# A hybrid decoder layer on one core: first steps in a fixed order, small products in larger groups, attention inputs between other projections

## The chip, the core and the metric

The kernel runs on one core of a Trainium2 chip, in one launch. The metric is the device time of a whole execution in microseconds (us). The core's engines are TensorE (PE in the profile; PEld is its weight load, PEq and SPq the sequencers), VectorE (DVE), ScalarE (ACT), GpSimd (POOL) and SyncE (SP), which here only issues DMAs. A step of the program becomes instructions in one queue per engine; an engine works its queue in order and waits on semaphores of the others.

## The reference

One decoder layer of width 1024 on one sequence of 256 tokens, all in float32:

```
h    = rms_norm(x, norm1_g)
proj = h @ w_in                                  # 1024 x (1824 + 1536 + 2048)
z    = token shift of proj[:1824]                # z + mu * (z of the token before - z)
y_a  = rwkv7_time_mix(z, ...)                    # 8 heads of 64: a recurrence over the tokens
q, k = partial_rope(rms_norm(.)); v              # from proj[1824:3360], 8 heads of 64
y_b  = softmax(causal q k^T / 8) v
g_a, g_b = sigmoid(proj[3360:])                  # two gates of 1024
x    = x + (g_a * (y_a @ w_branch_a) + g_b * (y_b @ w_branch_b)) @ w_out
x    = x + conv_ffn(rms_norm(x, norm2_g))        # up 1024 x 5632, conv of 3, gelu, down 2816 x 1024
```

The recurrence is, for each head, with a 64x64 state S: `S = S*w + (S a) b^T + v k^T`, `y = S r`, with w, a, b, k from the projections. Attention has blocks of 256 tokens, so with 256 tokens it is plain causal attention.

## The kernel before

**Weights and products.** All matrices of weights (some 68 MB) are read once, in tiles `raw` of 128 x 1024 (512 KB), by DMAs on SP's queue (`load_next`, L234), four buffers deep. Each tile is split into a high half `whi` in a shorter format of the same width, fp32r (`split_hi`, L239: a cast on ScalarE, L246, but for the first tile and those numbered 4 to 6, which VectorE casts: `HI_ENG`, L50), and a low half `wlo` (`split_lo`, L251, a subtraction on VectorE, L256). The activations are split in the same way into `hh` and `hl`. A product is then three: `hh`x`whi`, `hl`x`whi`, `hh`x`wlo`. `wst` (L275) has the weights stationary and 256 columns moving (L284, L286, L289), `xst` (L294) the activations stationary and 512 columns of weights moving (L305, L306, L309). These are called weight products below; a tile of weights gives 24 or 12 of them. Whoever takes a tile (`weights`, L261) also splits the next ones and so starts the next load.

**The first steps.** The gains of the norm (`p0`) and x come by DMA. ScalarE squares x, takes the root; VectorE takes the reciprocal `rs`, and x is multiplied by it (L333 to L342); TensorE transposes the result into PSUM (`xt`), from which ScalarE makes `hh` with the gains `par` as scale (L357) and VectorE `hl` (L358). `keep_warm` gives TensorE idle products (`idle`, L99). `ident` comes from an iota on POOL (L105). The other parameters follow: `p1` on SP's queue behind the first four weights, the rest on POOL's queue (`small_loads`), then the masks `gmask`, `cmask`, `m16`, `m32` and constants (`late_consts`, VectorE) and the tables of the rotation (`rope_tables`).

**Threads.** Up to branch 1 three kinds of work are merged. `bulk` (L949) makes the projections, each as one run of weight products: the decay and gate inputs first, then k, r, v of the recurrence, the three inputs of attention (`finish_qk` norms and rotates q and k), eight gates, and, when attention is done, branch 1. `chain` (L486) is the recurrence in four chunks of 64 tokens: decay (`pw`), normalisation of k (`pss`, `rx`, `prx`), the products of all chunks' keys with keys and queries (`pgr`, 8 heads x 4 chunks as 16 units x 2 halves of the partitions), masked into `G` (L595); then the inverse of a unit triangular matrix 64x64 for each unit. Its 16x16 diagonal blocks go through DRAM (`d`) into another layout, are inverted in fifteen steps on VectorE (L609 to L614) and come back through DRAM as `X` (L617, L623); two levels (`level`, L692) join them to 32 and 64. Meanwhile `pk`, `pv`, `pz0` prepare transposes and products that don't need `X`. Then the four chunks run one behind the other (`pz`, `pu`, `pS`, `pyt`), and `group_norm` (L733) follows each with `pc`. `attention` (L849) transposes q and k, makes the scores (`ps`), the softmax (L879 to L893), transposes it (`ppt`) and multiplies by v (`po`), in four parts: two halves of the tokens (t) by two halves of the heads (j), and writes `ybh` and `ybl`, which branch 1 takes (L917, L918).

**What sets the order.** `chain`, `bulk`, `attention` and `group_norm` are generators. Each `yield cost, latency` says how much of TensorE's time the step took and how long the thread should wait until its next one; the loop at L968 runs the first thread that is due, and `SLACK` scales the latencies. This gives the order in which instructions are written. A scheduler then may change each engine's order, by its own model, but for what `tc.issue_after` pins. A product of weights has 128 rows; most products of `chain` and `attention` have 64 rows on either half of the array, and the two kinds alternate on TensorE wherever a step of a thread falls between weight products.

After the threads come branch 0, the output projection and the MLP, which keep their code.

Of the kernel before, what the change touches and what calls it, by code (L numbers as in the profile page):

```python
# [9 lines left out]
F32 = mybir.dt.float32  # L10
# [8 lines left out]
S = 256  # L19
# [17 lines left out]
def body(tc, x, positions, norm1_g, w_in, rwkv_mu, w_decay_up, decay_bias, w_aaa_up,  # L37
# [5 lines left out]
    with ctx:  # L43
# [6 lines left out]
        HI_ENG = {i: dve for i in (4, 5, 6)}  # L50
# [37 lines left out]
        p0 = t1("p0", (8, 128))  # L88
        nc.gpsimd.dma_start(p0, rows(norm1_g, 8))
        x_sb = load_x()  # L90

        ones = cst.tile([128, 512], mybir.dt.bfloat16, name="ones")
        dve.memset(ones, 1.0)

        def keep_warm(n):

            p = acc("idle")
            for _ in range(n):
                pe.matmul(p, ones[:, 0:128], ones, start=True, stop=True)  # L99

        keep_warm(8)
        jp = t1("jp", (128, 128), I32)
        pool.iota(jp, pattern=[[1, 128]], base=0, channel_multiplier=-1)
        ident = cst.tile([128, 128], F32, name="ident")
        pool.tensor_scalar(ident, jp, 0.0, None, op0=OP.is_equal)  # L105
        eps1 = cst.tile([128, 2], F32, name="eps1")
        dve.memset(eps1[:, 0:1], NORM_EPS)
        dve.memset(eps1[:, 1:2], GN_EPS)
        warm = cst.tile([128, 1], F32, name="warm")
        act.activation(warm, eps1[:, 0:1], AF.Sqrt)  # L110
        jl = t1("jl", (128, 2, 64), I32)
        for q in range(2):
            pool.iota(jl[64 * q:64 * q + 64], pattern=[[0, 2], [1, 64]], base=0,
                      channel_multiplier=-1)
        p1 = t1("p1", (51, 128))
        p1_loads = []
        at = 0
        mu1 = rwkv_mu[0]
        for r, n in ((mu1[0:1792].rearrange("(n c) -> n c", c=128), 14),
                     (mu1[1696:1824].rearrange("(n c) -> n c", c=128), 1),  # L120
                     (rows(decay_bias, 4), 4), (rows(aaa_bias, 4), 4), (rows(k_k, 4), 4),
                     (rows(k_a, 4), 4), (r_k[0].rearrange("h n -> (h n)").rearrange("(n c) -> n c", c=128), 4),
                     (rows(ln_g, 4), 4), (rows(ln_b, 4), 4), (rows(norm2_g, 8), 8)):
            p1_loads.append((p1[at:at + n], r))
            at += n
        assert at == 51
        p2 = t1("p2", (88, 128))

# [8 lines left out]
        def late_consts():  # L137
            dve.tensor_scalar(gmask[:, 0:64], jl[:, 0], 0.0, None, op0=OP.is_gt)
            dve.tensor_scalar(gmask[:, 64:128], jl[:, 1], 0.0, None, op0=OP.is_ge)
            dve.memset(bones, 0.0)  # L140
            for q in range(2):
                dve.memset(bones[64 * q:64 * q + 64, 64 * q:64 * q + 64], 1.0)
            dve.tensor_reduce(rowf, ident.rearrange("p (a b c) -> p a b c", a=4, b=2)[:, :, 1, :],
                              axis=AX.XY, op=OP.add)
            dve.memset(m16, 0.0)
            dve.memset(m32, 0.0)
            for q in range(4):
                o = 32 * (q % 2)
                dve.memset(m16[32 * q:32 * q + 32, o:o + 16], 1.0)
                if q % 2:  # L150
                    dve.memset(m32[32 * q:32 * q + 32, 0:32], 1.0)
            dve.tensor_scalar(m16, m16, rowf, None, op0=OP.mult)
            dve.tensor_scalar(cmask, jp, 0.0, NEG, op0=OP.is_gt, op1=OP.mult)
            dve.memset(rst, 1.0)
            dve.memset(rst.rearrange("p (c i) -> p c i", i=64)[:, :, 0:1], 0.0)

# [3 lines left out]
        pt = atp("pt")  # L160
        pe.transpose(pt[:, 0:8], p0, ident[:8, :8])
        keep_warm(3)
# [3 lines left out]

        def late_params():
            pt = atp("pt")
            pe.transpose(pt[:, 0:51], p1, ident[:51, :51])
            pe.transpose(pt[:, 64:152], p2, ident[:88, :88])  # L170
            dve.tensor_copy(par[:, 8:59], pt[:, 0:51])
# [54 lines left out]

        queue, raws, halves, ready = [], [], [], []

        def load_next():
            if queue:  # L230
                ap = queue.pop(0)
                k, c = ap.shape[1], ap.shape[2]
# [892 lines left out]
```

## Time and profile before

| | us |
|---|---|
| runs | 438.62, 438.62, 439.71 (median 438.62) |
| the profiled execution | 438.61 |
| its span, first to last instruction | 436.8 |

| engine | busy of the span | instructions |
|---|---|---|
| PE (matmul) | 97% | 3600 |
| DVE | 69% | 545 |
| ACT | 56% | 391 |
| POOL | 3% | 21 |

The granted clock of TensorE is full in all 40 slices of the span. The core reads 68.76 MB at a mean of 161 GB/s. The times of the page and of the trace are counted from the span's start; of the 438.61 us, 1.8 lie around it. In a row of a group, `out<-in` names the tiles, then come the partitions x elements and the type, the count, the busy time with the mean of one in ns, and the idle time ahead of it with what ended most of it. Matmuls are pipelined, so the busy time of one is longer than the step from one to the next; where this matters, starts are compared. Where the costliest groups stand:

```profile
L284 PE MATMUL acc<-hh,whi 128*128 128x256 f32 x600 | 150.1, 284 | 1.7 <-ACT whi L246 0.8
L256 DVE TENSOR_TENSOR wlo<-raw,whi 128x1024 fp32r<-128x1024 f32 x125 | 152.2, 1219 | 53.1 <-PE acc L289 18.4
```

The first is one of the three kinds of weight products, 600 of them; the second the low halves on VectorE, which stood idle for 53.1 us before them.

### The profile page before, as it was taken

The page shows a single profiled execution, that of the slowest core. Times are in us where ns is not written, and L with a number is a line of the kernel's source. Part 1 is how long each engine was busy: PE and PEld are TensorE (multiplying, and loading weights), DVE is VectorE, ACT ScalarE, POOL GpSimd, SP SyncE. Part 2 cuts the span into 40 slices and gives each one's busy share as a digit, 9 for nine tenths or more (in the row PEclk, how much of TensorE's full clock was granted, in tenths as well). Part 3 has the DMA queues.
Part 4 walks back from the last instruction along what each step waited for, and adds up shares of the span by engine and source line. Part 5 has one row for each costly group of instructions (what it writes and reads, how often), then busy time and mean ns, then how long its engine had stood idle before and what let it go on. Part 6 is the DMA issues. An engine that isn't in the chain of part 4 may idle for free.

```text
span 436.8 us, 8837 instructions
## 1 busy us (share of the span) xinstructions
PE 425.6 (97%) x3600; PEld 384.0 (88%) x3600; DVE 301.4 (69%) x545; ACT 243.0 (56%) x391; POOL 12.8 (3%) x21
## 2 busy tenths in 40 slices
PE   7799998999999999999999999999999999999996
PEld 3688996788899989799997899999999999999995
DVE  4695899698456568676796479576576576576573
ACT  6489852644375446777355378455455455465450
POOL 6000040000000000000000000000000000000000
PEclk9999999999999999999999999999999999999999
DMA  8764836543657331164556366655665656565612
GB/s 234 195 190 125 243 94 195 132 129 54 194 154 230 95 104 51 50 190 127 166 182 195 107 211 184 226 189 166 200 192 178 195 193 191 191 182 185 214 50 96
DMA packets 62189, 70.76 MB, mean 162 GB/s; under 512 B 8898, under 2 KB 52617, under 8 KB 62150
## 3 DMA queue, kind: packets, MB, share of 16 engines
q1 hardware_dynamic: 61750, 69.50, 53.1%
q0 software_dynamic: 400, 0.71, 0.6%
q8 instruction: 28, 0.46, 0.4%
q14 instruction: 11, 0.09, 0.1%
HBM read 68.76 MB, written 1.44 MB: 161 GB/s over the span
## 4 chain that ended last, share of the span: by engine, by line
PE 82%; DVE 5%; ACT 5%; DMA 4%; issue 1%; SPq 1%; DVEq 0%; ACTq 0%
PE acc L284 15%; PE acc L286 15%; PE acc L289 15%; PE acc L305 4%; PE f L1045 4%; PE f L1043 4%; PE f L1044 4%; PE acc L306 4%; PE acc L309 4%; DMA raw<-in_w_in_dram 4%; DVE wlo L256 2%; ACT whi L246 1%; PE ps L876 1%; PE pp L704 1%; PE py L720 1%
## 5 line engine op out<-in xcount | busy, mean ns | idle before, releaser
L246 ACT CAST whi<-raw 128x1024 fp32r<-128x1024 f32 x121 | 126.4, 1050 | 119.3 <-PE acc L286 52.6
L256 DVE TENSOR_TENSOR wlo<-raw,whi 128x1024 fp32r<-128x1024 f32 x125 | 152.2, 1219 | 53.1 <-PE acc L289 18.4
L284 PE MATMUL acc<-hh,whi 128*128 128x256 f32 x600 | 150.1, 284 | 1.7 <-ACT whi L246 0.8
L286 PE MATMUL acc<-hl,whi 128*128 128x256 f32 x600 | 148.7, 282 | 0.9 <-DVE hl L358 0.9
L284 PEld LDWEIGHTS acc<-hh,whi 128*128 128x128 f32 x600 | 113.1, 188 | 4.4 <-ACT hh L357 1.5
L286 PEld LDWEIGHTS acc<-hl,whi 128*128 128x128 f32 x600 | 113.1, 188 | 3.2 <-DVE hl L358 1.5
L289 PE MATMUL acc<-hh,wlo 128*128 128x256 f32 x600 | 95.1, 281 | 1.2 <-DVE wlo L256 1.2
L289 PEld LDWEIGHTS acc<-hh,wlo 128*128 128x128 f32 x600 | 80.9, 189 | 2.1 <-DVE wlo L256 2.0
L1044 PE MATMUL f<-whi,hb 128*128 128x512 f32 x80 | 31.1, 389 | 0.0
L1043 PE MATMUL f<-whi,hb 128*128 128x512 f32 x80 | 31.1, 389 | 0.0
L1045 PE MATMUL f<-wlo,hb 128*128 128x512 f32 x80 | 31.1, 389 | 0.0
L305 PE MATMUL acc<-whi,hh 128*128 128x512 f32 x48 | 20.2, 425 | 0.0
L306 PE MATMUL acc<-whi,hl 128*128 128x512 f32 x48 | 18.8, 393 | 0.0
L1058 DVE TENSOR_TENSOR an<-acc,rsb 128x512 f32<-128x512 f32 x11 | 7.6, 691 | 14.8 <-PE acc L289 13.9
L1045 PEld LDWEIGHTS f<-wlo,hb 128*128 128x128 f32 x80 | 15.0, 188 | 3.1
L1044 PEld LDWEIGHTS f<-whi,hb 128*128 128x128 f32 x80 | 15.0, 188 | 2.7
L1043 PEld LDWEIGHTS f<-whi,hb 128*128 128x128 f32 x80 | 15.0, 188 | 2.7
L1076 DVE TENSOR_TENSOR cv<-cv,acc 128x256 f32<-128x256 f32 x22 | 8.3, 418 | 11.5 <-PE acc L289 11.2
L309 PE MATMUL acc<-wlo,hh 128*128 128x512 f32 x48 | 15.0, 393 | 0.0
L1065 ACT ACTIVATE cv<-an,cpar 128x256 f32<-128x256 f32 x22 | 12.0, 594 | 1.4 <-DVE an L1058 0.4
L305 PE MATMUL acc<-whi,mh 128*128 128x512 f32 x32 | 12.8, 399 | 0.0
L306 PE MATMUL acc<-whi,ml 128*128 128x512 f32 x32 | 12.6, 395 | 0.0
(274 smaller groups left out, 566.1 us busy)
## 6 DMA issues: line engine op xcount, KB each, us to landing
raw<-in_w_ffn_up_dram SPq DMA_DIRECT2D x44, 512.0 KB
raw<-in_w_in_dram SPq DMA_DIRECT2D x43, 512.0 KB
raw<-in_w_ffn_down_dram SPq DMA_DIRECT2D x22, 512.0 KB
raw<-in_w_out_dram SPq DMA_DIRECT2D x8, 512.0 KB
x<-in_x_dram SPq DMA_DIRECT2D x8, 256.0 KB
raw<-in_w_branch_b_dram SPq DMA_DIRECT2D x4, 512.0 KB
raw<-in_w_branch_a_dram SPq DMA_DIRECT2D x4, 512.0 KB
out_dram<-o SPq DMA_DIRECT2D x3, 256.0 KB
```

What stands on the lines that cost most here:

```text
L246: act.copy(hi[:, :k * c], raw[:, :k * c])
L256: dve.tensor_tensor(lo[:, :n], raw[:, :n], hi[:, :n].bitcast(F32), op=OP.subtract)
L284: pe.matmul(om, wh[:, k, ms], xh[:, k0 + k], start=k0 + k + m == 0, stop=False, skip_group_check=True)
L286: pe.matmul(om, wh[:, k, ms], xl[:, k0 + k], start=False, stop=False, skip_group_check=True)
L289: pe.matmul(om, wl[:, k, ms], xh[:, k0 + k], start=False, stop=k0 + k == nk - 1 and m == n - 1, skip_group_check=True)
L305: pe.matmul(ps_[t], xh[:, K, ts], wh[:, k], start=K == 0, stop=False)
L306: pe.matmul(ps_[t], xl[:, K, ts], wh[:, k], start=False, stop=False)
L309: pe.matmul(ps_[t], xh[:, K, ts], wl[:, k], start=False, stop=K == nk - 1)
L1043: pe.matmul(fin[f], hb[:, 0, i, ts], wh[:, 0, cs], start=st, stop=False)
L1044: pe.matmul(fin[f], hb[:, 1, i, ts], wh[:, 0, cs], start=False, stop=False)
L1045: pe.matmul(fin[f], hb[:, 0, i, ts], wl[:, 0, cs], start=False, stop=False)
L1065: act.activation(cv, pm, AF.Identity, scale=cpar[:, 44 + n:45 + n], bias=cpar[:, 66 + n:67 + n])
```

## The change

**The first steps** are written as one function, `first_steps`, under a fixed order (`tc.manual_schedule`) for PE, ACT, DVE and POOL. The factor `rs` of the norm is no longer multiplied into x: TensorE multiplies x by a diagonal matrix, `diag`, which transposes and scales in one. The gains and the first parameters come in one tile `p1` on POOL's queue (five issues), and no parameters go over SP's any more; the first weight tile is loaded in two halves. The order of the first weights' products is written out: high with `hh`, then `hl`, for four rows of weights, and their low halves behind; the first low half is made on POOL (`split_lo(pool)`), and `HI_ENG` is gone. The sigmoid's table is loaded ahead by a dummy. `late_consts` moves from VectorE to POOL, but for two instructions, `masks`, which are written in `chain`; the rest of the parameters are read out of `p2` by `late_params`, inside `chain`.

**Larger groups.** `pw`, `pgr`, `pk`, `pv`, `pz0` take four (`pv`, `pz0`: two) banks of PSUM at a time, and one step does what two or four did. `pk` now stands ahead of `pgr`. The two threads `level` become four joint steps for both halves. `pS` and `pyt` of a chunk are one step. `pc` of `group_norm` waits until a step of another thread than `bulk` has just been taken (`joined`). Attention does the first half of the tokens for all eight heads at once and the second half in two times four heads, and multiplies by v for each half of the tokens in one go (`weighted`).

**Order.** The inputs of attention stand between the other projections, and the first gate of branch 1 too; the planner's latencies are set anew, without `SLACK`.

```diff
-        HI_ENG = {i: dve for i in (4, 5, 6)}
+        joined = [False]
...
         def late_consts():
-            dve.tensor_scalar(gmask[:, 0:64], jl[:, 0], 0.0, None, op0=OP.is_gt)
...
+            pool.memset(rst, 1.0)
+            pool.memset(rst.rearrange("p (c i) -> p c i", i=64)[:, :, 0:1], 0.0)
+            pool.memset(wgu[0:96, 1], 0.0)
+            pool.memset(bones, 0.0)
             for q in range(2):
-                dve.memset(bones[64 * q:64 * q + 64, 64 * q:64 * q + 64], 1.0)
+                pool.memset(bones[64 * q:64 * q + 64, 64 * q:64 * q + 64], 1.0)
+            pool.tensor_scalar(gmask[:, 0:64], jl[:, 0], 0.0, None, op0=OP.is_gt)
+            pool.tensor_scalar(gmask[:, 64:128], jl[:, 1], 0.0, None, op0=OP.is_ge)
+            pool.tensor_scalar(cmask, jp, 0.0, NEG, op0=OP.is_gt, op1=OP.mult)
+            pool.memset(m16, 0.0)
+            pool.memset(m32, 0.0)
+            for q in range(4):
+                o = 32 * (q % 2)
+                pool.memset(m16[32 * q:32 * q + 32, o:o + 16], 1.0)
+                if q % 2:
+                    pool.memset(m32[32 * q:32 * q + 32, 0:32], 1.0)
+
+        def masks():
             dve.tensor_reduce(rowf, ident.rearrange("p (a b c) -> p a b c", a=4, b=2)[:, :, 1, :],
                               axis=AX.XY, op=OP.add)
...
             dve.tensor_scalar(m16, m16, rowf, None, op0=OP.mult)
...
-        queue += kh(win, 1536, 256) + kh(win, 1696, 128)
-        for c in (512, 768, 0, 256, 1024, 1280):
-            queue += kh(win, c, 256)
-        for i in range(3):
-            queue += kh(win, MOBA0 + 512 * i, 512)
...
+        for c, n in ((512, 256), (768, 256), (0, 256), (256, 256), (MOBA0, CW), (1024, 256), (1280, 256),
+                     (MOBA0 + CW, CW), (GATE0 + D, 256), (MOBA0 + 2 * CW, CW), (GATE0 + D + 256, 256),
+                     (GATE0 + D + 512, 256), (GATE0 + D + 768, 256)):
+            queue += kh(win, c, n)
...
+        def first_steps():
...
+            for i in range(NRAW):
+                load_next(i == 0)
...
+            keep_warm(8)
+            first_loads()
+            pool.iota(jp, pattern=[[1, 128]], base=0, channel_multiplier=-1)
+            pool.tensor_scalar(ident, jp, 0.0, None, op0=OP.is_equal)
...
+            small_loads(5)
...
+            for t in range(2):
...
+                act.activation(rs[:, t:t + 1], ss[:, t, 1:2], AF.Sqrt, scale=1.0 / D, bias=ss[:, t, 0:1])
+                dve.reciprocal(rs[:, t:t + 1], rs[:, t:t + 1])
+                diag = t1("diag", (128, 128))
+                dve.tensor_scalar(diag, ident, rs[:, t:t + 1], None, op0=OP.mult)
+                for k in (0, 2, 1, 3, 4, 6, 5, 7):
+                    pe.matmul(at(k)[:, t], x_sb[t][:, k * 128:k * 128 + 128], diag, start=True, stop=True)
+                if t == 0:
+                    pt = atp("pt")
+                    pe.transpose(pt[:, 0:31], p1, ident[:31, :31])
+                    early_params(pt)
+                    keep_warm(2)
...
+            for k in range(6):
+                high(k)
+            for k in range(2):
+                dve.tensor_copy(hi[:, k * 512:k * 512 + 512], raw[:, k * 512:k * 512 + 512])
+                low(k)
+            split_lo(pool)
+            small_loads(len(loads))
+            split_hi()
+            high(6)
+            high(7)
+            for k in range(2, 8):
+                low(k)
+            split_lo()
+            split_hi()
+            p = acc()
...
+            act.activation(warm, eps1[:, 0:1], AF.Sigmoid)
+            split_hi()
+            return p
...
+        with tc.manual_schedule(engines={E.PE, E.Activation, E.DVE, E.Pool}):
+            p = first_steps()
+        late_consts()
...
+            masks()
+            for g in range(2):
+                pg = [[p.rearrange("p (u i) -> p u i", u=4) for p in pj] for pj in banks("pgr")]
+                for ct in (2 * g, 2 * g + 1):
+                    for c in range(4):
...
+                for ct in (2 * g, 2 * g + 1):
+                    for q in range(2):
+                        dve.tensor_tensor(G[q][:, 4 * ct:4 * ct + 4], pg[ct % 2][q],
+                                          gmask[:, None, :].to_broadcast([128, 4, 128]), op=OP.mult)
...
-            for t, j in ((0, 0), (0, 1), (1, 0), (1, 1)):
...
+            p0 = yield from scores(0, 0, 8)
+            yield weighted(0, p0)
+            pa = yield from scores(1, 0, 4)
+            pb = yield from scores(1, 1, 4)
+            yield weighted(1, pa + pb)
...
-            for i in range(3):
+            def attention_input(i):
...
+            rope_tables()
+            yield from attention_input(0)
+            yield from proj4("v", 8)
+            yield from attention_input(1)
+            yield from gates(1, 0)
+            yield from attention_input(2)
+            threads.insert(1, ["att", attention(), now_t + 3.0])
+            for j in range(1, 4):
+                yield from gates(1, j)
+            for j in range(4):
+                yield from gates(0, j)
             while "att" not in done:
                 yield 0, 1.0
             yield from branch(1, *ybs)
...
-                th[2] = now_t + lat * SLACK.get(th[0], 1.0)
+                th[2] = now_t + lat
+                if cost:
+                    joined[0] = th[0] != "bulk"
```

In the changed kernel the prediction's line numbers L141, L143 (`masks`), L153 (`early_params`) and L366 to L393 (`first_steps`) are those of its own text.

513 lines of the change are left out of this document (225 added, 288 removed).

## The prediction

> **What bounds the kernel now.** I read the busy line, the chain of waits by engine, the stretches (length; busy time of PE, PEld, DVE, ACT and POOL with their instructions; granted clock, DMA share, GB/s), and then the order of time (start, duration, engine, line, work) on TensorE wherever it did something other than weight products.
>
> ```profile
> PE 425.6 (97%) x3600; PEld 384.0 (88%) x3600; DVE 301.4 (69%) x545; ACT 243.0 (56%) x391; POOL 12.8 (3%) x21
> PE 82%; DVE 5%; ACT 5%; DMA 4%; issue 1%; SPq 1%; DVEq 0%; ACTq 0%
> 0.00:25.00 25.00, 19.67 (x110) 14.03 (x110) 15.38 (x62) 14.87 (x30) 7.84 (x19) 1.00 0.73 202
> 25.00:110.00 85.00, 83.06 (x680) 71.82 (x681) 72.46 (x147) 53.25 (x86) 5.00 (x2) 1.00 0.54 146
> 110.00:207.00 97.00, 96.96 (x1233) 87.88 (x1233) 61.47 (x125) 58.90 (x110) 0.00 (x0) 1.00 0.45 132
> 207.00:437.00 230.00, 225.92 (x1580) 210.31 (x1579) 152.04 (x216) 115.93 (x166) 0.00 (x0) 1.00 0.56 176
> ```
>
> TensorE is busy from 25 us to the end and the chain runs through it for 82% of the span, so only what shortens its queue, or makes it wait, counts. The change touches the first three stretches; the last 230 us (branches, output projection, MLP) keep their code. The sum below is made against the profiled execution: span 436.8, time 438.6, which is also the median of the three runs (438.62).
>
> **Fewer, larger groups: a gain of 5.6 us.** What a group of small products costs beside its products is read where two sizes stand side by side.
>
> ```profile
> 75.76 0.62 PE L309 MATMUL acc<-wlo,hh 128*128 128x512 f32 x2
> 76.31 1.16 PE L592 MATMUL pgr<-AR,KB 64*128 64x128 f32 x16
> 77.40 0.51 PE L305 MATMUL acc<-whi,hh 128*128 128x512 f32 x1
> 78.45 0.62 PE L309 MATMUL acc<-wlo,hh 128*128 128x512 f32 x2
> 79.00 0.71 PE L634 MATMUL pk<-ident,KB 64*128 64x64 f32 x16
> 79.64 0.50 PE L305 MATMUL acc<-whi,hh 128*128 128x512 f32 x1
> 80.67 0.63 PE L309 MATMUL acc<-wlo,hh 128*128 128x512 f32 x2
> 81.22 0.46 PE L634 MATMUL pk<-ident,KB 64*128 64x64 f32 x8
> 81.62 0.50 PE L305 MATMUL acc<-whi,hh 128*128 128x512 f32 x1
> 68.72 0.62 PE L309 MATMUL acc<-wlo,hh 128*128 128x512 f32 x2
> 70.86 1.16 PE L592 MATMUL pgr<-AR,KB 64*128 64x128 f32 x14 [1.10 <-DVE G L595]
> 71.95 0.50 PE L305 MATMUL acc<-whi,hh 128*128 128x512 f32 x1
> ```
>
> A 512-wide weight product takes 0.23 us from start to start, so after the two that start at 78.45 the next was due at 78.90; it came at 79.64: 16 small products cost 0.74. After 80.67 it was due at 81.12 and came at 81.62: 8 cost 0.50. So one product costs 0.03 and going over to 64-row products and back 0.26. In the static order of TensorE's instructions, which I read for both kernels, such going over happens 36 times before the change (12 up to the inputs of the recurrence, 24 in recurrence and attention) and 20 times after it (6 and 14): 16 x 0.26 = 4.2 us. The products themselves are the same in number. The second of the four `pgr` groups also waits for VectorE to empty its PSUM: from 69.17 (due) to 71.95 it costs 2.78 against 1.19 (76.21 to 77.40) for the fourth. With four banks per group and thirty weight products between the two groups, VectorE's four multiplications are covered; 1.6 saved. The sixteen `pss` products, which stood partly one by one under weight products, come together: I charge 0.2. Bounds: nothing saved if every group waits for its input instead; 7 if changes inside a group vanish too.
>
> **The first steps: a loss of 1.0 us.** What the diff doesn't show, the static order does. Pinned are the instructions of `first_steps`; the constants are not, and the scheduler has set two mask instructions of `masks` in between. VectorE's order in the changed kernel:
>
> ```
> L369 reciprocal rs (t=0)
> L141 reduce rowf       waits for POOL
> L371 diag (t=0)
> L143 m16 = m16 * rowf  waits for POOL's 19th count: the last 32x16 memset of m16
> L153 copy par          (31 parameter columns)
> L366, L369 ss, rs (t=1); L371 diag (t=1); L393 high half of the first weights; L384 hl
> ```
>
> Behind L143 stand the norm gains, the second half of the norm and every `hl`. That memset is the 30th instruction or so of POOL's queue: ten DMA issues, two iotas, `ident`, the memsets of `rst`, `wgu`, `bones`, two `gmask`, `cmask`.
>
> ```profile
> 1.26 0.71 POOL L89 DMA_DIRECT2D p<-in_norm_g_dram  x1 [0.82 <-POOLq L1113]
> 2.47 0.58 POOL L105 TENSOR_SCALAR ident<-jp 128x128 f32<-128x128 int32 x1
> 3.31 0.62 POOL L188 DMA_DIRECT2D wdu<-in_w_decay_up_dram  x1
> 3.91 0.56 POOL L189 DMA_DIRECT2D wdu<-in_w_aaa_up_dram  x1
> 6.14 0.67 POOL L192 MEMSET wgu<- 96x512 f32 x1
> 58.91 3.25 POOL L572 TENSOR_TENSOR KB<-av,L 128x1024 f32<-128x1024 f32 x1 [47.51 <-DVE av L570]
> 7.08 0.15 DVE L404 COPY par<-pt 128x8 f32<-128x8 f32 x1
> 8.79 0.84 ACT L357 ACTIVATE hh<-xt,par 128x256 fp32r<-128x256 f32 x2 [0.29 <-PE xt L352]
> 10.08 0.35 PE L284 MATMUL acc<-hh,whi 128*128 128x256 f32 x1 [0.67 <-ACT hh L357]
> 0.00:23.60 23.60, 10.61 (x71) 1.00 0.75 210
> ```
>
> From 1.26: ten issues at 0.56 are 5.6; `rst` (1024 wide) an estimate of 0.9 from the 512-wide memset; `ident` 0.6, `wgu` 0.65; the integer masks, 256 columns together at `ident`'s rate, 1.2; iotas and some ten little memsets 1.6. That makes 11.8 us. Today the copy of the gains starts at 7.08 and `hh` at 8.79, 1.7 later; with the copy at 12.0 that is 13.7, and the first weight product some 0.5 after it, at 14.2 instead of 10.08. Then one more new wait: the low half of the first weights is POOL's (`split_lo(pool)`), which can start when VectorE has cast the second half (15.1) and takes the 3.25 of L572, so TensorE, whose order is pinned, waits at the end of its first sixteen products until 18.3. Eight low products (0.9), the second block (2.7) and the third (2.8) follow, and product 72 ends at 24.8. Before, the row of the first 23.6 us holds 71 of them. The loss is 1.0. That it isn't 4 is due to the old start's own waits, which go. Bounds: -2 if POOL's queue costs VectorE nothing (POOL's subtraction then starts at 12: 72 products at 21.9); +2.5 if its issues take 0.7 like the first.
>
> **ScalarE's share, two waits in the middle: a loss of 1.5 us.**
>
> ```profile
> 30.00:40.00 10.00, 10.00 (x90) 10.00 (x89) 5.62 (x8) 9.92 (x16) 0.00 (x0) 1.00 0.68 207
> 41.38 0.38 PE L284 MATMUL acc<-hh,whi 128*128 128x256 f32 x1 [0.75 <-ACT whi L246]
> L246 ACT CAST whi<-raw 128x1024 fp32r<-128x1024 f32 x121 | 126.4, 1050 | 119.3 <-PE acc L286 52.6
> L747 ACT ACT_TABLE_LOAD x4 | 5.1, 1283 | 0.1
> 78.22 3.30 SPq L602 DMA_DIRECT2D d<-G  x7
> 104.02 4.04 SPq L623 DMA_DIRECT2D X<-d  x8
> 119.74 0.55 PE L704 MATMUL pp<-X,G 64*64 64x64 f32 x9
> ```
>
> ScalarE is full from 30 to 40, and TensorE waits 0.75 for its cast just behind. Three casts that VectorE made (`HI_ENG`) come to it, 3 x 1.05 = 3.15; two table loads of 1.28 go, since the sigmoid's table is loaded early and serves the tanh too: +0.6 (bounds -0.9, the wait gone, and +3). The way from the first `d<-G` to the last `X<-d` took 30 us (78.22 to 108.06), and TensorE came for X 42 us after the last `pgr`. Now 150 weight products and 9 us of small ones lie between, 36 us, and the second attention input's normalisation (some 5 us of VectorE) runs among the fifteen steps of the inverse: 35 us are needed, and I charge 0.5 (0 to 3). The norm factors of k (`rx`) are wanted 44 products (5 us) after `pss`, with a table load and two casts ahead of them on ScalarE: 0.4 (0 to 1).
>
> **The end of attention: a loss of 5.5 us.** In the new static order the last weight product of the gate projections stands before the last groups, and branch 1 needs attention's output:
>
> ```
> pS pyt pyt pc ps pz | 24 weight products | pu pyt pc pyt ppt(8) po(16) | 2 products with ybh | pc | products with ybl
> ```
>
> So between the last scores (`ps`) and `ybl` TensorE has only these to do: `pz` 0.74, 24 x 0.116 = 2.8, and the small ones, 96 of 0.03, 8 transposes of 0.11, 32 wide ones of 0.05 with changes between, 6: together 9.5 us. What the same way takes today:
>
> ```profile
> 182.61 0.84 DVE L879 TENSOR_TENSOR sc<-ps,cmask 128x256 f32<-128x256 f32 x2 [1.03 <-PE ps L876]
> ...
> 190.05 0.66 PE L904 MATMUL ppt<-ident,sc 128*128 128x128 f32 x4
> 194.61 1.09 PE L913 MATMUL po<-pT,qkv 128*64 128x128 f32 x16
> 197.03 0.42 DVE L918 TENSOR_TENSOR ybl<-po,ybh 128x256 fp32r<-128x256 f32 x1 [0.53 <-ACT ybh L917]
> ```
>
> 14.8 us from 182.61 to the end of `ybl` at 197.45, all of it hidden. In the new order it is hardly shorter: the 7.4 to the first transpose stay, some 1.2 come before it for VectorE's share of the group norm, and behind it come the transposes 0.9, two copies of `pT` with a cast between 1.6, the rest of `po` 0.6, then on ScalarE a square, a table load of 1.28 and a root (2.0) that its order puts ahead of `ybh`, and `ybh` and `ybl` 1.3: 15.0. 15.0 - 9.5 = 5.5. Bounds: 1.5 (loads and group norm fit into handoffs) to 8.
>
> **The sum.** 438.6 - 5.6 + 1.0 + 0.6 + 0.5 + 0.4 + 5.5 = 441.0.
>
> **Rivals.** *The cover suffices.* Planner and scheduler may have left the end with slack that I don't see, its ScalarE work sliding ahead: then the last term is 0 to 1 and the time 435.5 to 436.5. The price is one wait at one place; everything else adds to -3.1, so it decides from a wait under 1.8 us. For it: in the row at 194.61 `po` waited for TensorE's order, not for its input. Against it: 7.4 us from scores to transposes aren't TensorE's. 0.32.
> *The order of the first steps costs nothing,* the mask's wait being over when VectorE gets there: -2 instead of +1, 438.0, no change that can be told. Against it: twelve us of POOL's queue; for it: its little memsets are no rows of this trace. 0.12.
> *The idle start slows what follows.* Early products run slower here:
>
> ```profile
> 1.46 4.88 PE L99 MATMUL idle<-ones 128*128 128x512 bf16 x11 [1.46 <-DVE eps L107]
> ```
>
> With its idle group's products 0.44 apart against 0.23 for as many columns later, TensorE is at half pace at first. In the new order it has nothing to do from about 8.5 to 13.2. [...] 0.14. [...]
>
> **How the numbers follow.** Forecast 0.42; 0.32, 0.12 and 0.14 for the rivals. A difference under 0.3% (1.3 us) can't be told from none: the three runs spread by 0.25%. Faster 0.32 (the first rival), same 0.12, slower 0.56. The forecast's own range, from its bounds taken as independent, is 438.5 to 444; with the first rival, which the second can take below 435, and the third it reaches from 434.0 to 445.5, which leaves out about 0.2.
>
> **What would show it.** Right: VectorE idle for some 5 us before L143, ended by POOL; the first weight product near 14; a wait of 2 us or more before the first `ppt` of the last group and another before the first product with `ybh`, 5 to 6 in all; `pgr` without a wait for `G`. Wrong: a first weight product before 10, the groups' costs unchanged at fewer groups, or the products with `ybh` following `po` at once.

## The result, and the profile after

The changed kernel is slower: 442.45 us, the median of five runs (441.5 to 443.35), against 438.62 before; the ratio is 1.0085, its 95% interval 1.0066 to 1.0103. The forecast was 441.0, range 434.0 to 445.5. The profiled execution took 442.45 with a span of 440.4; before it was 438.61 with 436.8. So 3.6 us of span are to be found.

The busy line and the chain of waits by engine of the changed kernel:

```profile
PE 423.8 (96%) x3614; PEld 389.6 (88%) x3614; DVE 292.7 (66%) x505; ACT 242.2 (55%) x388; POOL 26.1 (6%) x48
PE 86%; ACT 6%; DMA 2%; DVE 2%; issue 0%; DVEq 0%; POOL 0%; ACTq 0%
```

Its first three stretches:

```profile
0.00:25.00 25.00, 19.48 (x107) 15.69 (x108) 10.03 (x35) 13.88 (x27) 18.86 (x46) 0.93 0.64 182
25.00:110.00 85.00, 81.16 (x709) 74.01 (x708) 67.91 (x139) 52.25 (x86) 7.28 (x2) 0.98 0.56 157
110.00:207.00 97.00, 93.67 (x1200) 86.12 (x1199) 61.67 (x118) 58.54 (x108) 0.00 (x0) 0.98 0.44 126
```

TensorE is less busy in the second and third stretch (81.2 and 93.7 against 83.1 and 97.0), and a column that stood at 1.00 in every stretch before now reads 0.93, 0.98, 0.98: the granted clock. Three places show why. The first steps, in order of time on VectorE, POOL and TensorE:

```profile
5.96 0.28 DVE L371 TENSOR_SCALAR diag<-ident,rs 128x128 f32<-128x128 f32 x1
12.25 0.25 DVE L143 TENSOR_SCALAR m<-m,rowf 128x64 f32<-128x64 f32 x1 [6.01 <-POOL m L136]
12.42 0.18 DVE L153 COPY par<-pt 128x31 f32<-128x31 f32 x1
...
11.69 0.53 POOL L136 MEMSET m<- 32x16 f32 x4
17.00 2.39 POOL L247 TENSOR_TENSOR wlo<-raw,whi 128x1024 fp32r<-128x1024 f32 x1 [4.44 <-issue]
...
6.29 3.78 PE L373 MATMUL xt<-diag,x 128*128 128x128 f32 x16 [1.24 <-DVE diag L371]
13.62 3.23 PE L373 MATMUL xt<-diag,x 128*128 128x128 f32 x16 [2.49 <-DVE diag L371]
16.50 0.77 PE L411 MATMUL acc<-hh,whi 128*128 128x256 f32 x2
```

VectorE stands still for 6.0 us before the mask instruction, released by POOL's memset, and the gains are copied at 12.4. POOL itself, whose low half waits for the first weights' high half, stands still for 4.4 until 17.0. The first weight product comes at 16.5, not at 10.1. Then the second place, on VectorE, ScalarE and TensorE:

```profile
30.91 0.17 DVE L197 CAST posf<-posi 128x2 f32<-128x2 int32 x1 [4.24 <-DMA posi<-in_positions_dram]
31.26 1.22 DVE L247 TENSOR_TENSOR wlo<-raw,whi 128x1024 fp32r<-128x1024 f32 x1
...
31.18 1.05 ACT L237 CAST whi<-raw 128x1024 fp32r<-128x1024 f32 x1 [2.42 <-DMA raw<-in_w_in_dram]
42.54 1.03 ACT L237 CAST whi<-raw 128x1024 fp32r<-128x1024 f32 x1
...
43.63 0.39 PE L275 MATMUL acc<-hh,whi 128*128 128x256 f32 x1 [3.20 <-ACT whi L237]
```

VectorE waits 4.2 us for the positions, the last load of POOL's queue, with a low half of weights behind it. ScalarE waits 2.4 for its next tile, and from the start of that cast to the next one on ScalarE 11.4 us go by, with other work. TensorE waits 3.2. The chain of work that ended last (start, length, what) runs through ScalarE's row, not through VectorE's wait:

```profile
22.66 8.49 DMA raw<-in_w_in_dram
...
31.18 1.05 ACT whi L237
...
42.64 0.94 ACT whi L237
```

The tile of the first of these casts was asked for at 22.66, before VectorE's wait began at 26.7, and took 8.5 us to land. From 22.6 to 31.2 the DMA engines are 98% busy: five tiles asked for between 19.4 and 26.4 share them with the ten loads that POOL issues from 19.35 on (the expectations count nine). VectorE's row ends close behind; in the profile of e3 below, the chain goes through the positions. Third, the end of attention on TensorE:

```profile
194.46 0.65 PE L773 MATMUL pc<-ident,yc 64*64 64x64 f32 x14 [0.76 <-DVE yc L766]
198.12 1.58 PE L917 MATMUL ppt<-ident,sc 128*128 128x128 f32 x8 [1.89 <-DVE sc L908]
199.62 3.10 PE L930 MATMUL po<-pT,qkv 128*64 128x128 f32 x32
203.41 0.50 PE L275 MATMUL acc<-ybh,whi 128*128 128x256 f32 x2 [0.69 <-ACT ybh L934]
```

And behind each of the three, the clock (stretches of the changed kernel, with the same columns as above):

```profile
14.60:17.70 3.10, 3.10 (x17) 3.10 (x16) 1.65 (x5) 2.62 (x7) 0.69 (x1) 0.50 0.00 0
...
45.00:48.00 3.00, 3.00 (x15) 3.00 (x16) 3.00 (x5) 3.00 (x7) 0.00 (x0) 0.50 0.65 171
49.00:52.00 3.00, 3.00 (x29) 3.00 (x28) 3.00 (x4) 2.15 (x4) 0.00 (x0) 1.00 0.96 324
...
199.00:202.00 3.00, 3.00 (x26) 2.67 (x26) 1.40 (x5) 2.97 (x6) 0.00 (x0) 0.50 0.00 0
```

TensorE is busy all through 45 to 48 and starts 15 products there; from 49 to 52 it starts 29. Each stretch at 0.50 follows a standstill, of 2.49, 3.20 and 1.89 us.

Where the span went, summed over both traces from the starts of weight products (what a step is longer than 0.1135 us, or 0.227 for 512 columns, is put to the place where it lies):

| | before | after | difference | forecast |
|---|---|---|---|---|
| start of the 72nd weight product | 23.6 | 25.8 | +2.2 | +1.0 |
| groups of small products, waits in the last one taken out | 60.2 | 54.1 | -6.1 | -5.6 |
| waits and half clock in the last group of attention | - | 5.0 | +5.0 | +5.5 |
| waits and half clock between weight products, from there to about 60 us | 2.6 | 7.2 | +4.6 | +1.5 |
| small delays elsewhere | 14.1 | 12.0 | -2.1 | 0 |

The third row is the three waits (0.76, 1.89, 0.69) and half clock: `ppt` took 1.58 and `po` 3.10, where e8 below, without it, took 1.09 and 1.97.

### The profile page after: what moved, and what is told of

The parts are those of the page before. It is cut to its first block, busy times and chain, and to the rows that moved or that the text cites. A ratio compares the mean times of both kernels' runs of the same rounds, so it can differ in the third digit from the quotient of the medians.

```text
span 440.4 us, 8868 instructions
## 1 busy us (share of the span) xinstructions
PE 423.8 (96%) x3614; PEld 389.6 (88%) x3614; DVE 292.7 (66%) x505; ACT 242.2 (55%) x388; POOL 26.1 (6%) x48
## 3 DMA queue, kind: packets, MB, share of 16 engines
HBM read 68.76 MB, written 1.44 MB: 159 GB/s over the span
## 4 chain that ended last, share of the span: by engine, by line
PE 86%; ACT 6%; DMA 2%; DVE 2%; issue 0%; DVEq 0%; POOL 0%; ACTq 0%
PE acc L275 16%; PE acc L280 16%; PE acc L277 16%; PE acc L296 4%; PE acc L300 4%; PE acc L297 4%; PE f L1077 4%; PE f L1076 4%; PE f L1078 4%; DMA raw<-in_w_in_dram 2%; PE px L726 1%; ACT whi L237 1%; PE pp L710 1%; PE pgr L610 1%; PE po L930 1%; PE ppt L917 1%
## 5 line engine op out<-in xcount | busy, mean ns | idle before, releaser
L237 ACT CAST whi<-raw 128x1024 fp32r<-128x1024 f32 x124 | 129.8, 1050 | 132.0 <-PE acc L277 71.3
L275 PE MATMUL acc<-hh,whi 128*128 128x256 f32 x584 | 146.1, 285 | 3.2 <-ACT whi L237 3.2
L277 PE MATMUL acc<-hl,whi 128*128 128x256 f32 x584 | 143.5, 281 | 0.0
L275 PEld LDWEIGHTS acc<-hh,whi 128*128 128x128 f32 x584 | 110.7, 190 | 5.5 <-ACT whi L237 3.4
L277 PEld LDWEIGHTS acc<-hl,whi 128*128 128x128 f32 x584 | 110.7, 190 | 0.5
L280 PE MATMUL acc<-hh,wlo 128*128 128x256 f32 x584 | 92.8, 282 | 0.9 <-DVE wlo L247 0.8
L280 PEld LDWEIGHTS acc<-hh,wlo 128*128 128x128 f32 x584 | 79.4, 191 | 1.5 <-DVE wlo L247 1.5
L296 PE MATMUL acc<-whi,hh 128*128 128x512 f32 x48 | 19.3, 403 | 0.0
```

Source lines behind the costliest of these rows:

```text
L237: act.copy(hi[:, :k * c], raw[:, :k * c])
L275: pe.matmul(om, wh[:, k, ms], xh[:, k0 + k], start=k0 + k + m == 0, stop=False, skip_group_check=True)
L277: pe.matmul(om, wh[:, k, ms], xl[:, k0 + k], start=False, stop=False, skip_group_check=True)
L280: pe.matmul(om, wl[:, k, ms], xh[:, k0 + k], start=False, stop=k0 + k == nk - 1 and m == n - 1, skip_group_check=True)
L296: pe.matmul(ps_[t], xh[:, K, ts], wh[:, k], start=K == 0, stop=False)
```

## The experiments

All compare with the kernel before on the same chip; the ratio of the changed kernel is 1.0085. A difference of ratios times 438.6 gives microseconds.

| kernel | median us | ratio to before, 95% interval | span of its profile |
|---|---|---|---|
| changed | 442.45 | 1.0085 (1.0066 to 1.0103) | 440.4 |
| e1 mask late | 438.90 | 1.0013 (0.9999 to 1.0027) | 434.6 |
| e2 positions first | 440.74 | 1.0048 (1.0022 to 1.0075) | 436.7 |
| e3 idle filled | 440.62 | 1.0061 (1.0038 to 1.0084) | 439.8 |
| e4 attention earlier | 437.89 | 0.9982 (0.9965 to 0.9998) | 435.8 |
| e5 three together | 433.71 | 0.9877 (0.9843 to 0.9911) | 431.9 |
| e6 one cast back | 431.00 | 0.9817 (0.9791 to 0.9844) | 427.1 |
| e7 old groups | 438.75 | 0.9995 (0.9971 to 1.0020) | 435.5 |
| e8 end filled | 440.98 | 1.0050 (1.0030 to 1.0070) | 439.6 |
| e9 old groups spaced | 431.89 | 0.9838 (0.9818 to 0.9858) | 430.1 |
| e10 first low on VectorE | 439.72 | 1.0013 (0.9997 to 1.0029) | 438.1 |
| e11 cast alone | 440.39 | 1.0039 (1.0025 to 1.0052) | 437.5 |
| e12 low and rope pinned | 430.57 | 0.9810 (0.9788 to 0.9832) | 429.1 |

**e1, the mask late.** `first_done` holds the last VectorE instruction of the first steps.

```diff
-            masks()
+            with tc.issue_after(first_done[0]):
+                masks()
```

> The changed kernel with one order edit: the two mask instructions (rowf, and m16 times rowf) may only come on VectorE after the first steps. Theory: m16 times rowf, which waits 6.0 us for POOL there, holds up the gains, the second half of the norm, the first weights' high half and with it POOL's low half and POOL's later loads. Without it TensorE goes on at 11.1 with the second half of x, the first weight product starts near 14.7 (16.5 now), the third block ends near 23.2 (26.0 now), TensorE's clock stays granted in full there, and the time falls by 2.5 to 4 us, to 438.5 to 440. Rival: POOL's low half of the first weights sets the pace of the pinned products whatever VectorE does; then the first product comes earlier, but the third block ends within 1 us of 26.0 and the time falls by less than 1.

It took 3.2 us off. (The profile is that of its fastest execution, 436.58.) Rows of TensorE, VectorE and again TensorE:

```profile
9.68 2.05 PE L374 MATMUL xt<-diag,x 128*128 128x128 f32 x16 [0.75 <-DVE diag L372]
...
26.66 0.17 DVE L198 CAST posf<-posi 128x2 f32<-128x2 int32 x1 [3.96 <-DMA posi<-in_positions_dram]
...
38.78 0.45 PE L276 MATMUL acc<-hh,whi 128*128 128x256 f32 x1 [2.57 <-ACT whi L238]
```

The second half of x starts 3.9 us earlier, the first weight product comes at 11.5, and no half clock follows the standstill of 0.75. The theory holds, but 1.7 of the 3.9 are luck of this execution: its first sixteen products with `diag` took 2.05 in place of 3.78 (last section). In e5, with the same edit, they took 3.61, and the first weight product comes at 13.4. The wait for the positions is still 4.0, only earlier with all the rest: the mask isn't what makes the second place.

**e2, the positions first.**

```diff
-        loads.append((posi, positions[0].rearrange("(t p) -> p t", p=128)))
+        loads.insert(5, (posi, positions[0].rearrange("(t p) -> p t", p=128)))
```

> The changed kernel with the load of the token positions put first among the nine loads that POOL issues behind its low half (19.4 in place of 24.2); the first 19 us keep their order. Theory: VectorE's conversion of the positions waits 4.2 us for this load (26.7 to 30.9) with a low half of weights behind it, which makes a weight tile, ScalarE's cast of it and all ScalarE work behind late, and TensorE's wait of 3.2 us before 43.6 is the end of this. The wait at 30.9 falls to under 1, the waits between 37 and 44 (0.6 and 3.2) to 1.5 in all, half clock behind them goes, and the time falls by 3 to 4.5 us, to 438 to 439.5. Rival: ScalarE is late from its own work, since three casts came to it; then the wait before 43.6 stays over 2.5 and the time falls by less than 1.

1.6 us less, between theory and rival. VectorE no longer waits for the positions (first row, no idle time), and TensorE's wait falls from 3.2 to 1.2 without half clock behind it:

```profile
27.29 0.16 DVE L197 CAST posf<-posi 128x2 f32<-128x2 int32 x1
...
41.46 0.39 PE L275 MATMUL acc<-hh,whi 128*128 128x256 f32 x1 [1.24 <-ACT whi L237]
```

The way is not that of the theory: ScalarE's cast comes earlier because its tile, asked for at 23.02, still before VectorE gets to the positions, took less time to land.

```profile
23.02 5.96 DMA raw<-in_w_in_dram
```

With the positions last (the changed kernel, e1, e3, e4, e8, e11) this tile took 7.2 to 8.8 us, with the positions first (e2, e5, e6, e7, e9) 6.0 to 7.5, and 4.9 and 5.0 in e10 and e12, where POOL's loads are all issued by 17.7. So POOL's loads seem to slow the tile; that, and why their order counts, was not tried alone. The executions differed, though: three of ten took 438.4 to 438.9 (mean clock 0.992; the profile is of one of them), five took 441.3 to 442.9 (0.984 to 0.988). What made the difference was not shown: there is no trace of one of the five. ScalarE's own part was left to e5, e6 and e11.

**e3, the standstill filled with idle products.**

```diff
-                    keep_warm(2)
+                    keep_warm(7)
```

> The changed kernel with seven in place of two idle products on TensorE between the two halves of x, so that it works from 10.3 to 13.3 where it now stands still from 11.1 to 13.6; nothing else moves. Theory: the granted clock of 0.5 from 14.6 to 17.7 follows from that standstill; filled, the clock stays at 1.0, the first weight product comes at about 15.3 (16.5 now), but POOL's low half, which is not TensorE's, comes at 18.8 to 19.4 as now, so that the third block ends at most 0.7 earlier, and the time falls by 0 to 1 us. Rival: the clock drops for another reason (TensorE's first work on full-size tiles); then nothing changes.

```profile
10.27 1.88 PE L107 MATMUL idle<-ones 128*128 128x512 bf16 x7
13.64 2.05 PE L373 MATMUL xt<-diag,x 128*128 128x128 f32 x16 [1.49 <-DVE diag L371]
```

The stretch that was at half clock, here:

```profile
14.60:17.70 3.10, 2.78 (x22) 2.38 (x22) 1.99 (x5) 3.10 (x8) 1.03 (x1) 1.00 0.00 0
```

The causes stayed, the clock did not fall (1.00 where it was 0.50), and the first weight product came 1.05 us earlier, at 15.45; the 72nd came only 0.3 earlier, since TensorE now waits longer for POOL's low half, as expected (it stands still for 0.69 between 18 and 20, for 0.33 in the changed kernel). The time fell by 1.05, but the two intervals overlap. So half clock did follow from this standstill; what it costs the whole execution here can't be told from noise.

**e4, attention earlier.**

```diff
-                th[2] = now_t + lat
+                th[2] = now_t + lat * (0.7 if th[0] == 'att' else 1.0)
```

> The changed kernel with the attention thread's latencies in the planner times 0.7; the code of the first steps and of the recurrence stays, 72 groups in the static order in place of 66 count both kinds. The last scores stand 48 weight products ahead of their transposes in place of 24, and 36 products lie between the last po and branch 1 in place of none. Theory: the end of attention costs 5.0 us now (waits of 0.8, 1.9 and 0.7 and about 1.6 of half clock behind them); with the cover no wait over 0.5 is left there, three more groups cost 0.8, and the time falls by 3.5 to 4.5 us, to 438 to 439. Rival: the softmax is late because VectorE and ScalarE are, so that the wait comes back elsewhere; then the time falls by less than 1.5.

4.5 us less, as the theory had it. The end of attention in this kernel, stretches:

```profile
190.00:212.00 22.00, 22.00 (x237) 20.94 (x234) 14.15 (x27) 12.79 (x18) 0.00 (x0) 1.00 0.55 171
```

TensorE is busy throughout, at full clock. One number of the planner made nearly the whole of this loss (4.5 of 5.0).

**e8, the end filled.** Nine idle products into the bank of the last transposes; the causes of the waits stay.

```diff
                     pp = atp("ppt")
+                    if (t, j, g) == (1, 1, 0):
+                        for _ in range(9):
+                            pe.matmul(pp, ones[:, 0:128], ones, start=True, stop=True)
```

> The changed kernel with nine idle products (512 columns each, into the bank that the transposes then use) on TensorE in its waits at the end of attention, three before pc, one between, five before the transposes; the waits' causes stay. Theory: half clock from 198.8 to 202.0 follows from TensorE's standing still for 0.8 and then 1.9 us, and costs 1.2 to 1.6; with the holes filled no stretch of half clock lies there, and the time falls by 0.8 to 1.6 us against the changed kernel, to about 440.9 to 441.7. Rival: half clock comes with the wide products of the transposes or is not what counts there: the time stays within 0.5 of 442.45.

```profile
198.58 1.09 PE L920 MATMUL ppt<-ident,sc 128*128 128x128 f32 x8 [0.27 <-DVE sc L908]
199.91 1.97 PE L933 MATMUL po<-pT,qkv 128*64 128x128 f32 x32 [0.24 <-ACT pT L921]
203.10 0.50 PE L275 MATMUL acc<-ybh,whi 128*128 128x256 f32 x2 [1.22 <-ACT ybh L937]
```

1.5 us less (the intervals overlap at their ends), and no half clock there; in the traces the way from `pu` to the first product with `ybh` is 0.8 shorter. The wait before `ybh` grew from 0.7 to 1.2, since ScalarE was not faster: part of what the clock gives back ends in the next wait.

**e5, the three order edits together** (e1, e2 and e4).

> The three order edits together: mask late, positions first, attention's latencies times 0.7. Theory: they mend three separate places (the start, the wait near 40, the end of attention), so their gains of about 3.4, 1.8 and 4.5 us against the changed kernel add up to most of their sum: 432.5 to 435, faster than before by 0.8 to 1.4%. The first weight product comes near 11.5, the wait at 36 to 40 is 1.4 at most, no wait over 0.5 stands before ybl. Rival: the first two are one chain (mask late, POOL late, positions late), so that doing both gives no more than the first alone: 434.5 to 436.

9.1 us less than the changed kernel (0.0208 x 438.6), where the three alone sum to 9.3: they add up. But the wait near 38 did not shrink to 1.4:

```profile
27.03 1.05 ACT L238 CAST whi<-raw 128x1024 fp32r<-128x1024 f32 x1 [1.03 <-DMA raw<-in_w_in_dram]
...
31.33 1.28 ACT L219 ACT_TABLE_LOAD   x1
32.87 1.28 ACT L511 ACT_TABLE_LOAD   x1
38.40 1.03 ACT L238 CAST whi<-raw 128x1024 fp32r<-128x1024 f32 x1
...
39.48 0.38 PE L276 MATMUL acc<-hh,whi 128*128 128x256 f32 x1 [2.25 <-ACT whi L238]
```

VectorE waits for no load here. The tile of the first cast landed at 27.01, after 7.0 us, and still 11.4 us lie from one cast to the next on ScalarE: eight sigmoids, two table loads, exponentials and `kp`. So the positions were not the only cause.

**e6, one cast back on VectorE**, on top of e5.

```diff
         def split_hi(eng=act):
             if raws:
+                eng = dve if nhi[0] in (6,) else eng
+                nhi[0] += 1
```

> The three edits together, and the seventh cast (number 6) of those that go through split_hi is VectorE's, as it was before the change. Theory: what is left of the wait near 38 (1.4 us with the positions first) is ScalarE's own order, eight sigmoids, two table loads and six other operations between two casts; with one cast on VectorE the wait falls to 0.5 or less and the time lies 0.5 to 1.2 us under that of the three edits alone. Rival: the wait is for ScalarE's zk or for VectorE just behind, and the cast moves it by less than 0.3 us: the same time within 0.3.

2.6 us less than e5 (the intervals just touch), more than the theory had, since the half clock behind the wait (40.5 to 43.9 in e5) went too. From 30 to 42 us TensorE has no wait at all, its busy share of the span is 98%, and its granted clock 1.00:

```profile
PE 417.4 (98%) x3614; PEld 383.3 (90%) x3614; DVE 293.5 (69%) x506; ACT 240.1 (56%) x387; POOL 26.3 (6%) x48
```

**e11, the same cast in the changed kernel alone.**

> The changed kernel with the one cast (number 6) on VectorE and nothing else. Theory: at the wait before 43.6 (3.2 us) ScalarE is late for two reasons that come one behind the other, VectorE's wait for the positions before it and its own eight sigmoids, two table loads and six more operations between two casts; with the cast taken out of that row the wait falls under 1.5, the half clock behind it goes, and the time falls by 2 to 4 us, to 438.5 to 440.5. Rival: with the positions late, VectorE is just as late with the cast as ScalarE was: less than 1 us.

2.0 us less. The wait of 3.2 for the cast is gone, and the half clock behind it; what is left there is this wait for a low half:

```profile
39.15 0.74 PE L284 MATMUL acc<-hh,wlo 128*128 128x256 f32 x4 [1.09 <-DVE wlo L251]
```

So the cast pays with the positions late, too. (For the first of the two reasons in the expectation, the chain of the changed kernel shows the late tile in place of VectorE's wait.)

**e7 and e9, the old group sizes** for `pgr`, `pv` and `pz0`, on e5 and, with planner latencies that keep the end in its place, on e6.

```diff
-            for g in range(2):
-                pg = [[p.rearrange("p (u i) -> p u i", u=4) for p in pj] for pj in banks("pgr")]
+            for ct in range(4):
+                pg = [chp("pgr").rearrange("p (u i) -> p u i", u=4) for q in range(2)]
```

> The three edits together, with the sizes of before for pgr, pv and pz0 (four and two and two groups; pk stays one): five more goings over to small products, and two banks in place of four for pgr. Prediction's price: 5 x 0.26 = 1.3 us for the groups and 1.6 for pgr's wait for VectorE, so 2.5 to 3 us more than the three edits alone, 435 to 438. Rival: a going over costs nothing that can't be hidden and the pgr wait came from the work around it before: within 0.7 us of the three edits alone.

5.2 us more than e5 (0.0118 x 438.6), above both. The profile shows a new wait: branch 0 now waits for the group norm, with half clock behind (0.94 from 208 to 210, 0.50 from 210 to 212); the recurrence ends later in the static order.

```profile
210.00 1.01 PE L276 MATMUL acc<-yah,whi 128*128 128x256 f32 x3 [2.43 <-ACT yah L777]
```

That confounds the price of the groups. (There are four more of them, not the five of the expectation.)

> Once more the sizes of before for pgr, pv and pz0, now on the kernel of the three edits with one cast on VectorE, and with latencies in the planner by which the end of the recurrence and of attention keeps its place in the static order (96 products and the last pc ahead of branch 0, as without the old sizes; four more groups, 12 or 6 products apart). Theory: four goings over more at 0.26 are 1.0 us, and VectorE keeps up with two banks when it isn't late: 431.6 to 432.8 against 431.0, and no new wait in the trace; the other 4 us of the first try were a wait of 2.65 before branch 0 and the half clock behind it. Rival: the groups of before are dearer in themselves (a wait for G at the second pgr, as in the old kernel): 433.5 to 436.

```profile
73.39 1.16 PE L615 MATMUL pgr<-AR,KB 64*128 64x128 f32 x16
77.43 1.25 PE L615 MATMUL pgr<-AR,KB 64*128 64x128 f32 x16
```

0.9 us more than e6 (0.0021 x 438.6; the intervals overlap, so the time alone does not settle it), and in the trace each group of 16 takes 1.2 of TensorE's time where one of 32 takes 2.1: up to the next weight product the price of a going over is as forecast (2 x 1.2 - 2.1 = 0.3). No `pgr` waits for `G`. VectorE comes to the first `G` 2.2 us after its group, as late as in the old kernel (2.4), but 12 or more weight products lie between the groups here and six there.

**e10 and e12, the first low half on VectorE**, on e6; in e12 the tables of the rotation are held behind the first steps too.

```diff
-            split_lo(pool)
+            split_lo()
...
-            rope_tables()
+            with tc.issue_after(first_done[0]):
+                rope_tables()
```

> The three edits with one cast on VectorE, and the first weights' low half made on VectorE in place of POOL. Theory of the prediction: POOL's low half makes TensorE wait before its first low products (0.9 us at 14.7 there), and POOL's loads wait behind it; on VectorE it takes 1.2 in place of 2.4, but stands ahead of six hl, each of which then comes 1.2 later. The two cancel to within 0.5: 430.5 to 431.5. Rival: POOL's part is what sets the start: 1 us less.

8.6 us more than e6, far from both. In this kernel the scheduler put the positions' conversion ahead of the gains, between pinned instructions:

```profile
15.14 0.24 DVE L198 CAST posf<-posi 128x2 f32<-128x2 int32 x1 [8.94 <-DMA posi<-in_positions_dram]
```

> The kernel before (three edits, one cast and the first low half on VectorE) with the tables of the rotation, too, held behind the first steps on VectorE. Theory: the 8 us lost there were not VectorE's low half, but the conversion of the positions, which the scheduler had put ahead of the gains on VectorE and which waited 8.9 us for its load; held back, the first weight product is back near 11.5 and the time is that of the kernel with POOL's low half within 0.7: 430.3 to 431.7. Rival: nine loads that POOL now issues early crowd out the first weights, or the low half on VectorE costs by itself: 433 or more.

430.57: the same as e6 within the intervals. It was the order, not the engine of the low half. e6 and e12 beat both kernels, by 1.8 and 1.9% against before.

## Why the prediction held, and where it was off

**Sign and mechanism at both ends were right.** Two of the reasons given for a slower kernel are each enough to take the loss away: without the mask's wait (e1) the changed kernel is level with before, with attention earlier (e4) it is slightly faster.

**Groups: -5.6 forecast, -6.1 found.** Price of a going over up to the next weight product, 0.26: the trace of e9 bears it out. The second part, 1.6 for `pgr`'s wait, went as said; e9 adds that spacing alone would have removed it. But the price was read too short, as the kernel before shows behind its last `pgr`:

```profile
77.40 0.51 PE L305 MATMUL acc<-whi,hh 128*128 128x512 f32 x1
77.75 0.40 PE L306 MATMUL acc<-whi,hl 128*128 128x512 f32 x1
77.98 0.39 PE L305 MATMUL acc<-whi,hh 128*128 128x512 f32 x1
```

The step from the first weight product to the second is 0.35, the next 0.23. Such a step, some 0.11 longer than the others, stands behind the groups of small products in both traces, 48 times before and 27 times after the change. That is 1.8 of the 2.1 us of the table's last row, so that a going over costs 0.37 and the groups gave 7.9.

**First steps: +1.0 forecast, +2.2 found.** VectorE's release was put at 11.8 and came at 12.25. Mis-sized was the way from the gains to the first weight product, 2.2 in the forecast (12.0 to 14.2) and 4.1 in the trace: it was read off a second half of x that was transposed in 1.1 (before: eight products from 8.32), while sixteen products with `diag` take 2.05 at full clock (e3) and took 3.23 here, at half clock from 14.26. POOL's low half, taken at 3.25, took 2.39; that gave some of it back.

**ScalarE and the middle: +1.5 forecast, +4.6 found.** This is the step that failed. The text charged 0.6 for the casts, with a bound of 3, and 0.9 for waits for `X` and `rx` that did not come. (The table loaded for the sigmoid at 19.98 did serve the tanh, at 25.18 without a load between; before, each had its own, at 21.62 and 24.87.) What came instead is one wait of TensorE with several causes in a row (the chains of the changed kernel and e2, then e5, e6 and e11): a tile that took 8.5 us to land beside POOL's late loads, ScalarE's eleven microseconds between two casts, and half clock behind; VectorE's wait for the positions runs close beside it. The forecast followed POOL's queue only as far as VectorE's first steps. It listed nowhere the ten loads behind the low half, whose end it had itself put at 18.3, nor that the last of them brings the positions.

**End of attention: +5.5 forecast, +5.0 found**, in other parts than given: 3.3 of waits, where the forecast had 5 to 6, and 1.6 of half clock, which it had only in a rival. That the sums agree is luck.

**The rival of the idle start** was given 0.14 as a case of its own. It is no alternative: half clock came with the forecast's waits, at three places, the start among them. The upper end of the range, 445.5, rests on a term for it that no run shows. What the runs showed in its place is half clock for 3.41 us at each of the three, behind waits of 1.89 to 3.20 (last section); filling the hole took 1.0 off at the start (e3) and 1.5 at the end of attention (e8), both hardly clear of noise.

That the whole came within 1.5 us of the forecast is in part luck: the first steps and the middle missed by +4.3, the other rows by -3.1.

## What to carry to other kernels

Where part of a program is pinned and the rest is not, read each engine's final order around the pinned part: an unpinned instruction that waits for a slow queue stops all that is pinned behind it (6.0 us here, 8.9 in e10). Follow such a queue to its end, too: its late loads share the DMA engines with the weights (98% busy here). A wait of TensorE can cost more than itself: with the waits of 1.89, 2.49 and 3.20 us of the changed kernel came half clock, 1.6 us more at the end of attention, and idle products in the hole kept the clock full (e3, e8). Larger groups pay by the number of goings over (0.37 us each); the planner's latencies around them, which fix what covers the last wait, were worth more here (4.5 us for one factor).

## What the runs showed of the hardware that was not expected

In these traces half clock lasted 3.41 us, or two or three times that. In the clock records of the changed kernel it is 3.41 each time, from 14.26 to 17.67, from 44.98 to 48.39 and from 198.58 to 201.99. Taken from the granted clock of stretches of 1 us, it lasts 3.40 to 3.42 in e1, e2, e3, e5, e7, e8 and at one place of e10, but 6.82 in e11 (11.84 to 18.66) and 10.24 at the other place of e10 (12.02 to 22.26).

In the changed kernel it began 0.64, 1.35 and 0.46 us behind the end of a wait of TensorE, of 2.49, 3.20 and 1.89. In the others it came with waits of 2.57 in e1, 2.84 in e2, 2.25 in e5, 2.43 in e7, 2.75 in e8, 2.47 and 6.61 in e10 and 4.00 in e11. With waits of 1.49 in e3, 1.24 in e2, 1.10 before the change, 1.09 in e11 and 0.75 in e1 the clock stayed at 1.00. What sets the length, and from what wait on half clock comes, was not shown.

The start is another matter. The first sixteen products with `diag`, behind 1.2 us of standstill in both, took 3.78 us in the profile of the changed kernel and 2.05 in that of e1:

```profile
6.17 2.05 PE L374 MATMUL xt<-diag,x 128*128 128x128 f32 x16 [1.16 <-DVE diag L372]
```

The stretches give a granted clock of 1.00 for both, but they only take off half clock that is recorded, and the clock records begin at 10.84 us in the changed kernel and at 7.31 before the change. Up to there products come at half pace: those with `diag` 0.21 us apart in place of 0.11 in the changed kernel, and before the change the transposes of `xn` 0.21 apart at 7.16 and 0.11 from 7.46 on. In the other traces the same sixteen took 2.05 (e6, e7, e10, e11) or 3.60 to 3.78 (e2, e3, e4, e5, e8, e9, e12), behind 1.13 to 1.44 and 1.13 to 1.66 us of standstill. So at the start the wait does not tell which of the two it is; between them lie 1.7 us of the first steps.
